# Windowed attention with its values as the stationary operand, in high and low parts, and outputs feature-major

## The chip, the cores and the metric

The kernel runs on one core of a Trainium2 chip. The metric is the device time of one execution in microseconds (us); the smaller is the better.

## The reference, cut to what matters

Two blocks follow each other on 512 tokens of 1024 features, all in fp32. The first ends in a large expert layer. The second begins with the layer that is changed here, a windowed attention with 16 heads of 64 features that share 4 key and value heads:

```python
u = rms_norm_2(h, norm_g[0])
q, k, v, z = jnp.split(u @ w_in, [1024, 1280, 1536], axis=-1)
logits = einsum(q, k) * scale - slopes * dist
logits = where(valid, logits, NEG_BIG)
probs = softmax(concatenate([logits, sink_col]))[..., :-1]
o = einsum(probs, v)
h = h + (o * silu(z)) @ w_out
```

A block of 128 queries sees its own block of 128 keys and the one on each side, so of four query blocks two see 2 key blocks and two see 3: 10 pairs of blocks per head. A gated embedding step and a second, different attention layer (called B below) follow.

## The kernel before

Almost every product of the kernel is fp32 split in a high and a low part of the type fp32r, and three matmuls (high by high, and two mixed ones) give the result. `linear_tm` and `linear_fm` are these products for a whole weight, in panels of two blocks of rows, which a helper loads, copies (`whi`, ACT, L148) and subtracts (`wlo`, L149). With `by_part` they run one output block at a time, in 24 matmuls of 512 columns (L153 to L155), and call `then` after each part. `to_fm` (L137 to L140) turns 128 tokens feature-major: eight transposes on TensorE (PE), in groups of four, each copied by ScalarE (ACT) and subtracted by VectorE (DVE).

A list scheduler with a timeline of its own fixes the order on every engine ahead of time; on the chip each engine works in its order, and waits there.

The stretches that matter here come in this order:

- **The tail.** The expert layer's last matmuls of token blocks 1 to 3 (`add_out`, L794 to L799, 512 columns each) end while VectorE and the others finish block 0. `make_u(t)` norms 128 tokens for layer A and turns them by `to_fm`. `make_u(0)` is called ahead of the tail (L860), `make_u(1)` and so on from inside it.
- **V, K and Q.** `linear_tm` for the values (into `vA`), `linear_fm` for the keys (`khA`, `klA`) and the first 8 heads' queries (`qA`).
- **Heads 0 to 7.** `linear_fm` for the other 8 heads' queries in four parts; after each, two heads.
- **Heads alone.** Heads 8 to 10, with what the scheduler leaves of the two heads before and takes of the next: the work of some five heads. So six are left in the three periods before, and five in the gates.
- **Gates.** `linear_tm` for z in eight parts of 24 matmuls, and after each of five parts a head. `gate_a` makes z times its sigmoid from a tanh (`th`), and multiplies it into `oA` (L1013).
- **Out.** `to_fm` of the four rows of `oA`, then the out projection.

One head is `a_head` (L951 to L990). For each of the four query blocks `t`: two matmuls give the logits (L965, L966, 384 or 256 columns, the PSUM tile `lg`), VectorE adds `abias` and takes the maximum (L969, the operation CUSTOM_DVE_ANT_0, into one of three buffers `L`), negates it (L972), ScalarE takes the exponential and its sum (L973), TensorE transposes each key block (L976, PSUM `tp`), one copy brings them to SBUF (`pt`: L979 on VectorE for odd blocks of the first 8 heads, otherwise L981 on ScalarE), and one fp32 matmul of 64 columns per key block (L983) has a block of `pt` as the stationary operand and `vA` as the moving one. So there are 10 transposes and 10 such matmuls per head, 160 and 160 in all, and each of these matmuls stands as two in the profile. At the end VectorE makes the reciprocal of the sums (L987, L988) and scales the head's four blocks with it into `oA` (L989), which is token-major.

Layer B's head (`b_head`, L1146 to L1176) does the last step in another way: its probabilities are split in `ph` and `pl` (L1163, L1164), its values are the stationary operand, high and low parts side by side, and 256 columns of probabilities move (L1170).

Of the kernel before, what the change touches and what calls it, by code (L numbers as in the profile page):

```python
# [91 lines left out]
def block_kernel(ctx: ExitStack, tc: tile.TileContext, A, out):  # L92
# [743 lines left out]
    for n in range(P):  # L836
# [17 lines left out]
        if n == P - WS - 1:  # L854
            assert turn == 2 * NSLOT
            g2 = ada_row(5)
            uT, make_u = normed_parts("norm_g_2", 0)
            nc.vector.tensor_mul(y, y, g2)
            nc.vector.tensor_add(x[:, 0], x[:, 0], y)
            make_u(0, "lg")  # L860

    for t in range(NG):
        for i, ops in enumerate(tail):
            add_out(t, ops, False, i == WS - 1)
        res = gp.tile([P, D], FT, name="res", tag="g", bufs=GB)
# [59 lines left out]
    klA = lz.tile([P, 4, S], FR, name="klA", tag="klA")  # L925
    vA = lz.tile([P, NT, 256], FT, name="vA", tag="vA")
    oA = lz.tile([P, NT, D], FT, name="oA", tag="oA")

# [17 lines left out]

    linear_tm(Wa, 8, 1280, 256, uT, NT, lambda t, p: nc.scalar.activation(vA[:, t], p, AF.Copy), by_part=True,
              then=lambda t: t == NT - 2 and make_u(NT - 1, "lg"))
    linear_fm(Wa, 8, 1024, 256, uT, NT, evac_ka)

    def a_head(h, q):  # L951
        abias = lw.tile([P, 3 * P], FT, name="abias")
        nc.vector.scalar_tensor_tensor(abias, dist[:, 0], -(2.0 ** (-8.0 * (h + 1) / 16.0)), dist[:, 1],
                                       op0=OP.mult, op1=OP.add)
        sm = small.tile([P, 3, NT], FT, name="sm3", tag="sm3")
        o = ps.tile([P, 512], FT, name="acc", tag="acc", bufs=4)
        for t in range(NT):
            sl = slice(t * P, (t + 1) * P)
            b_lo, b_hi = max(0, t - 1), min(NT - 1, t + 1)
            nb = b_hi - b_lo + 1  # L960
            n = nb * P
            c0 = (b_lo - (t - 1)) * P
            lg = ps.tile([P, 512], FT, name="lg", tag="lg")
            ks = slice(b_lo * P, (b_hi + 1) * P)
            nc.tensor.matmul(lg[:, :n], q[:, sl], khA[:, h // 4, ks], start=True, stop=False)  # L965
            nc.tensor.matmul(lg[:, :n], q[:, sl], klA[:, h // 4, ks], start=False, stop=True)  # L966
            L = lw.tile([P, 3 * P], FT, name="L", bufs=3)
            m = small.tile([P, 1], FT, name="m", tag="m")
            nc.vector.tensor_tensor_reduce(out=L[:, :n], in0=lg[:, :n], in1=abias[:, c0:c0 + n], scale=1.0,  # L969
                                           scalar=sink[:, h:h + 1], op0=OP.add, op1=OP.max, accum_out=m)  # L970
            nm = sm[:, 0, t:t + 1]
            nc.vector.tensor_scalar(nm, m, -1.0, None, op0=OP.mult)  # L972
            nc.scalar.activation(L[:, :n], L[:, :n], AF.Exp, bias=nm, accum_out=sm[:, 1, t:t + 1])  # L973
            p = ps.tile([P, 4, P], FT, name="tp", tag="tp")
            for b in range(nb):
                nc.tensor.transpose(p[:, b], L[:, b * P:(b + 1) * P], ident)  # L976
            pt = lw.tile([P, 3, P], FT, name="pt", bufs=3)
            if h < 8 and t % 2:
                nc.vector.tensor_copy(pt[:, :nb], p[:, :nb])  # L979
            else:  # L980
                nc.scalar.activation(pt[:, :nb], p[:, :nb], AF.Copy)  # L981
            for b in range(nb):
                nc.tensor.matmul(o[:, t * 64:(t + 1) * 64], pt[:, b],  # L983
                                 vA[:, b_lo + b, (h // 4) * 64:(h // 4 + 1) * 64], start=b == 0, stop=b == nb - 1)
# [46 lines left out]
    ple_split(0, lz.tile([P, 2, S], FT, name="pT", tag="vA"), pf)  # L1031
    _, make_n = normed_parts("ple_norm_g_2", 0, nT)
# [231 lines left out]
```

## Time and profile before

| | |
|---|---|
| time, median of 3 runs | 2329.86 us (2329.52 to 2330.2) |
| the profiled execution | 2336.29 us |
| its span | 2334.1 us |
| mean granted clock of TensorE | 0.984 |
| PE busy | 2241.3 us, 96% |
| DVE busy | 1623.3 us, 70% |
| ACT busy | 1114.2 us, 48% |
| POOL busy | 1051.2 us, 45% |

The span is what the profiler shows of the execution; 2.2 us lie around it. PE is TensorE, POOL GpSimd, SP the engine that issues most transfers. A matmul's duration in the rows overlaps the next one's, so two starts tell more than a duration. PEclk, or granted clock, is 1.00 at 2.4 GHz and 0.50 at 1.2 GHz.

### The profile page before, as it was taken

To read this page: it belongs to the slowest core of one execution; us is meant where nothing else is said; L and a number is where in the kernel's file an instruction comes from. 1 tells how busy PE (TensorE), PEld (TensorE's weight loads), DVE (VectorE), ACT (ScalarE), POOL (GpSimd) and SP (SyncE) were. 2 spreads that over 40 slices of the span, in tenths; PEclk is the share of its full clock that TensorE was granted. 3 is DMA by queue.
4 is the path that set the end of the run, shared out by engine and by line. 5 is a ranking of instruction groups with operands and counts; after the bars stand their busy time and mean duration, and the time that the engine had idled before them with its cause. 6 is when DMAs were issued, how large, how long until landed. Compare 5 with 4: busy or idle time off the path is not lost.

```text
span 2334.1 us, 32581 instructions
## 1 busy us (share of the span) xinstructions
PE 2241.3 (96%) x11610; PEld 1930.8 (83%) x11610; DVE 1623.3 (70%) x2962; ACT 1114.2 (48%) x2134; POOL 1051.2 (45%) x642
## 2 busy tenths in 40 slices
PE   7999999998999899999999999999999999989998
PEld 5777778988999899999997788887889789767676
DVE  7695447889585654888887988888565445347755
ACT  3656323436757675333332333333456444467742
POOL 4874034574545565778876655564110100121100
PEclk9999999999999999999999999999999999999999
DMA  7465122376767788999998999996410233211121
GB/s 277 145 204 184 60 77 79 124 236 207 257 244 259 247 297 308 341 342 342 334 336 303 340 327 342 327 336 234 129 39 18 82 108 97 74 49 53 33 82 63
DMA packets 206482, 463.04 MB, mean 198 GB/s; under 512 B 17680, under 2 KB 99056, under 8 KB 203248
## 3 DMA queue, kind: packets, MB, share of 16 engines
q1 hardware_dynamic: 169456, 326.72, 41.9%
q0 software_dynamic: 36864, 134.23, 15.8%
q8 instruction: 92, 1.51, 0.3%
q14 instruction: 70, 0.57, 0.1%
HBM read 415.26 MB, written 44.58 MB: 197 GB/s over the span
## 4 chain that ended last, share of the span: by engine, by line
PE 70%; DVE 9%; DMA 6%; issue 6%; POOL 4%; ACT 3%; SPq 0%; POOLq 0%; DVEq 0%; ACTq 0%
PE acc L155 16%; PE acc L154 16%; PE acc L153 15%; PE gp L680 3%; PE tp L155 2%; PE tp L154 2%; PE tp L153 2%; PE lg L154 2%; PE lg L153 2%; PE lg L155 2%; DMA g<-in_peer_v_dram,idx 2%; PE lg L1154 2%; DVE oh L666 1%; POOL wada L271 1%; POOL wlo L716 1%
## 5 line engine op out<-in xcount | busy, mean ns | idle before, releaser
L716 POOL TENSOR_TENSOR wlo<-wraw,whi 128x1024 fp32r<-128x1024 f32 x172 | 441.7, 2570 | 397.0 <-ACT whi L715 388.2
L715 ACT ACTIVATE whi<-wraw 128x1024 fp32r<-128x1024 f32 x256 | 268.9, 1051 | 153.5 <-PE lg L154 73.2
L153 PE MATMUL acc<-fm,whi 128*128 128x384 f32 (+2 forms) x932 | 333.3, 359 | 1.6 <-ACT av L728 1.3
L155 PE MATMUL acc<-fm,wlo 128*128 128x384 f32 (+2 forms) x932 | 322.5, 348 | 3.0 <-POOL wlo L716 2.9
L154 PE MATMUL acc<-fm,whi 128*128 128x384 f32 (+2 forms) x932 | 323.1, 347 | 0.0
L751 DVE CUSTOM_DVE_ANT_0 g<-g,h20y 128x1024 f32<-128x1024 f32 x128 | 197.5, 1548 | 120.5 <-DMA g<-in_peer_u_dram,idx 120.3
L790 ACT ACTIVATE wh<-w 128x384 fp32r<-128x384 f32 x128 | 67.2, 525 | 360.2 <-DVE w L787 345.1
L148 ACT ACTIVATE whi<-wraw 128x1024 fp32r<-128x1024 f32 (+5 forms) x142 | 138.4, 981 | 160.4 <-PE acc L155 89.2
L149 POOL TENSOR_TENSOR wlo<-wraw,whi 128x1024 fp32r<-128x1024 f32 (+4 forms) x48 | 104.4, 2183 | 240.1 <-ACT whi L148 231.5
L154 PE MATMUL acc<-wlo,wh 128*128 128x512 f32 x512 | 203.7, 398 | 5.1 <-POOL wlo L716 5.1
L761 DVE SCALAR_TENSOR_TENSOR h20y<-g,act,h20y 128x1024 f32<-128x1024 f32 x127 | 192.5, 1516 | 17.7 <-DMA g<-in_peer_v_dram,idx 17.2
L155 PE MATMUL acc<-whi,wl 128*128 128x512 f32 x512 | 204.0, 398 | 0.0
L153 PEld LDWEIGHTS acc<-fm,whi 128*128 128x128 f32 x932 | 178.3, 192 | 11.6 <-issue 2.2
L149 DVE TENSOR_TENSOR wlo<-wraw,whi 128x1024 fp32r<-128x1024 f32 (+3 forms) x94 | 109.2, 1169 | 113.1 <-ACT whi L148 109.5
L155 PEld LDWEIGHTS acc<-fm,wlo 128*128 128x128 f32 x932 | 177.7, 191 | 11.4 <-POOL wlo L716 4.2
L154 PEld LDWEIGHTS acc<-fm,whi 128*128 128x128 f32 x932 | 178.4, 192 | 9.0 <-issue 2.2
L734 POOL DMA_INDIRECT g<-in_peer_u_dram,idx x128 | 172.9, 1351 | 26.5 <-issue 14.5
L734 POOL DMA_INDIRECT g<-in_peer_v_dram,idx x128 | 160.7, 1255 | 34.6 <-issue 21.5
L153 PE MATMUL acc<-whi,wh 128*128 128x512 f32 x512 | 171.7, 396 | 0.5 <-ACT whi L715 0.4
L669 ACT ACTIVATE oh<-oh,gT 128x128 f32<-128x128 f32 x384 | 120.1, 392 | 77.4 <-DVE oh L666 77.2
L153 PE MATMUL acc<-whi,fm 128*128 128x512 f32 (+3 forms) x368 | 135.9, 375 | 3.3 <-ACT fm L139 2.1
L791 DVE TENSOR_TENSOR wl<-w,wh 128x384 fp32r<-128x384 f32 x128 | 113.2, 884 | 35.9 <-ACT wh L790 33.9
(367 smaller groups left out, 5512.8 us busy)
## 6 DMA issues: line engine op xcount, KB each, us to landing
wraw<-in_uT_dram SPq DMA_DIRECT2D x128, 512.0 KB
wraw<-in_peer_v_dram SPq DMA_DIRECT2D x128, 512.0 KB
wada<-in_w_adaT_dram SPq DMA_DIRECT2D x48, 512.0 KB
G_d<-stage SPq DMA_DIRECT2D x24, 1024.0 KB
gm<-G_d SPq DMA_DIRECT2D x64, 384.0 KB
A_d<-av SPq DMA_DIRECT2D x88, 192.0 KB
am<-A_d SPq DMA_DIRECT2D x88, 192.0 KB
wraw<-in_w_in_dram SPq DMA_DIRECT2D x24, 512.0 KB
```

Of the source, the lines that this page charges most:

```text
L148: nc.scalar.activation(hi[:, :nk, :n], raw[:, :nk, :n], AF.Copy)
L149: eng.tensor_sub(lo[:, :nk, :n], raw[:, :nk, :n], hi[:, :nk, :n].bitcast(FT))
L153: nc.tensor.matmul(o, lh, rh, start=first, stop=False)
L154: nc.tensor.matmul(o, lh, rl, start=False, stop=False)
L155: nc.tensor.matmul(o, ll, rh, start=False, stop=last)
L669: nc.scalar.activation(oh[:, 1, i], oh[:, 1, i], AF.Copy, scale=gT[:, q * 4 + i:q * 4 + i + 1])
L715: nc.scalar.activation(hi, raw, AF.Copy)
L716: eng.tensor_sub(lo, raw, hi.bitcast(FT))
L734: tc.keep_in_program_order(nc.gpsimd.indirect_dma_start(out=g, out_offset=None, in_=src, in_offset=bass.IndirectOffsetOnAxis(ap=idx0[:, s: ...
L751: nc.vector.tensor_tensor_reduce(out=g, in0=g, in1=h20, scale=1.0, scalar=0.0, op0=OP.mult, op1=OP.add, accum_out=act0[:, i:i + 1])
L761: nc.vector.scalar_tensor_tensor(y, g, act0[:, s:s + 1], y, op0=OP.mult, op1=OP.add)
L791: nc.vector.tensor_sub(wl, w, wh.bitcast(FT))
```

## The change

- `make_u(0)` moves from ahead of the tail into it, behind `add_out` of its second token block.
- The values are stored in two parts, high and low, 64 columns each side by side (`evac_va`): a ScalarE copy, and a VectorE subtraction that is new.
- In `a_head` two query blocks go together. All transposed probabilities are copied by ScalarE to `ph`, and VectorE subtracts them to `pl` (L992). A half head then takes six matmuls of type fp32r, two for each of three key blocks: values (128 columns, high and low) by `ph`, and values (64 columns, high) by `pl`, over 256, 128 and 256 moving columns. That is 12 per head and 192 in all.
- Their output is feature-major, high products on partitions 0 to 63, low ones on 64 to 127. ScalarE copies the upper half (`ol`), VectorE adds it to the lower into `oA`, now feature-major. The reciprocals go to `rs`, unapplied.
- `gate_a` multiplies `rs` into z instead of z into `oA`. `gated_a` transposes z (four transposes per 128 features, 32 in all) and multiplies it into `oA`. Eight ScalarE copies and eight VectorE subtractions then make the parts for the out projection, in place of `to_fm`, which had as many of each.
- `th` is now a buffer of the tag of the gains.

```diff
-            make_u(0, "lg")
 
     for t in range(NG):
         for i, ops in enumerate(tail):
             add_out(t, ops, False, i == WS - 1)
+        if t == 1:
+            make_u(0, "lg")
...
+    vA = lz.tile([P, NT, 4, P], FR, name="vA", tag="vA")
+    oA = lz.tile([P, 8, S], FT, name="oA", tag="oA")
+    rs = lz.tile([P, NT, A_HEADS], FT, name="rs")
+
+    def evac_va(t, p):
+        v = p.rearrange("p (h d) -> p h d", d=64)
+        nc.scalar.activation(vA[:, t, :, 0:64], v, AF.Copy)
+        nc.vector.tensor_sub(vA[:, t, :, 64:128], v, vA[:, t, :, 0:64].bitcast(FT))
...
+        for t0 in (0, 2):
+
+            b0 = max(0, t0 - 1)
+            ph, pl = [lw.tile([P, 3, 2 * P], FR, name=n) for n in ("ph", "pl")]
+            for t in (t0, t0 + 1):
...
+                nc.scalar.activation(ph[d], p[:, :nb], AF.Copy)
+                nc.vector.tensor_sub(pl[d], p[:, :nb], ph[d].bitcast(FT))
+
+            for i, (b, u0, u1) in enumerate(((0, 0, 2), (2, 1, 2), (1, 0, 2)) if t0 == 0 else
+                                            ((2, 0, 2), (1, 0, 1), (3, 0, 2))):
+                c, w = slice((t0 + u0) * P, (t0 + u1) * P), (slice(None), b - b0, slice(u0 * P, u1 * P))
+                v = vA[:, b, h // 4]
+                steps = [(o[:, c], v, ph[w]), (o[0:64, c], v[:, 0:64], pl[w])]
+                for n in ((0, 1), (1, 0))[i == 2]:
+                    nc.tensor.matmul(*steps[n], start=i == 0 and n == 0, stop=i == 2 and n == 0)
+        ol = tmp.tile([64, S], FT, name="ol", tag="h", bufs=2)
+        nc.scalar.activation(ol, o[64:128], AF.Copy)
+        nc.vector.tensor_add(oA[h % 2 * 64:h % 2 * 64 + 64, h // 2], o[0:64], ol)
         es = sm[:, 2]
         nc.scalar.activation(es, sm[:, 0], AF.Exp, bias=sink[:, h:h + 1])
         nc.vector.tensor_add(es, es, sm[:, 1])
-        nc.vector.reciprocal(es, es)
-        nc.vector.tensor_mul(oA[:, :, h * 64:(h + 1) * 64], o[:, :NT * 64].rearrange("p (t d) -> p t d", d=64),
-                             es[:, :, None].to_broadcast([P, NT, 64]))
+        nc.vector.reciprocal(rs[:, :, h], es)
...
-        th = lw.tile([P, 512], FT, name="th")
+        th = tmp.tile([P, 512], FT, name="th", tag="gain", bufs=2)
...
-            c = slice(j * 512, (j + 1) * 512)
-            nc.vector.tensor_mul(oA[:, i, c], oA[:, i, c], zA[:, i, c])
+            z = zA[:, i, j * 512:(j + 1) * 512].rearrange("p (h d) -> p h d", d=64)
+            nc.vector.tensor_mul(z, z, rs[:, i, 8 * j:8 * j + 8, None].to_broadcast([P, 8, 64]))
+
+    def gated_a(k):
+
+        p = ps.tile([P, 4, P], FT, name="tp", tag="tp")
+        for t in range(NT):
+            nc.tensor.transpose(p[:, t], zA[:, t, k * P:(k + 1) * P], ident)
+        nc.vector.tensor_mul(oA[:, k], oA[:, k], p.rearrange("p t s -> p (t s)"))
...
+                  then=lambda t, j=j: (one_head(11 + 4 * j + t), j and t < 2 and [gated_a(2 * t + i) for i in (0, 1)]))
+    for k in range(4, 8):
+        gated_a(k)
     aT = fm_whole()
-    for t in range(NT):
-        to_fm(oA[:, t], 8, aT, t)
+    for k in range(8):
+        nc.scalar.activation(aT[0][:, k], oA[:, k], AF.Copy)
+        nc.vector.tensor_sub(aT[1][:, k], oA[:, k], aT[0][:, k].bitcast(FT))
```

The scheduler makes a new order of it on every engine. Three places follow, in the order of issue.

TensorE, in the heads that stand alone, before: `lg` is a logit tile, `tp` a tile of transposes, L983 the fp32 product of probabilities and values.

```order
L965 MATMUL lg<-khA,qA 128x384
L966 MATMUL lg<-klA,qA 128x384
L976 MATMUL tp<-ident,L 128x128 x2
L983 MATMUL acc<-vA,pt 128x64 x3
L965 MATMUL lg<-khA,qA 128x256
L966 MATMUL lg<-klA,qA 128x256
L976 MATMUL tp<-ident,L 128x128 x2
L983 MATMUL acc<-vA,pt 128x64 x2
```

And after the change, where L1000 is the new product, and L978, L979 and L989 are the lines of the logits and transposes:

```order
L989 MATMUL tp<-ident,L 128x128 x4
L1000 MATMUL acc<-ph,vA 128x256
L978 MATMUL lg<-khA,qA 128x256
L979 MATMUL lg<-klA,qA 128x256
L978 MATMUL lg<-khA,qA 128x384
L979 MATMUL lg<-klA,qA 128x384
L1000 MATMUL acc<-pl,vA 64x256
L1000 MATMUL acc<-ph,vA 128x128
L1000 MATMUL acc<-pl,vA 64x128
L1000 MATMUL acc<-pl,vA 64x256
L1000 MATMUL acc<-ph,vA 128x256
L989 MATMUL tp<-ident,L 128x128 x6
```

The transposes now stand in groups of 4 and 6 in turn, and each group stands behind the five matmuls of a half head, of which three read `pl`.

VectorE, in the heads that stand alone, before, from a negation to the next head's `abias` (ISA is CUSTOM_DVE_ANT_0, and its second row reads the maximum out; L1008 is of the gates):

```order
L972 TENSOR_SCALAR sm_16113<-m 128x1
L969 ISA L,m<-lg,abias,sink 128x384
L969 ISA m 128x1
L969 ISA L,m<-lg,abias,sink 128x256
L969 ISA m 128x1
L1008 SCALAR_TENSOR_TENSOR zA<-th,zA 128x512
L989 TENSOR_TENSOR oA<-acc,sm_15987 128x4x64
L972 TENSOR_SCALAR sm_16113<-m 128x1 x2
L953 SCALAR_TENSOR_TENSOR abias<-dist 128x384
```

And after, where L1003 is the sum of the two halves of a head's output and L992 the subtraction to `pl`:

```order
L1003 TENSOR_TENSOR oA<-acc,ol 64x512
L985 TENSOR_SCALAR sm_15992<-m 128x1
L1007 RECIPROCAL rs<-sm_15992 128x4
L992 TENSOR_TENSOR pl<-tp,ph 128x3x128 x2
L982 ISA L,m<-lg,abias,sink 128x384
L982 ISA m 128x1
L982 ISA L,m<-lg,abias,sink 128x256
L982 ISA m 128x1
L992 TENSOR_TENSOR pl<-tp,ph 128x2x128
L985 TENSOR_SCALAR sm_16072<-m 128x1
L992 TENSOR_TENSOR pl<-tp,ph 128x2x128
L985 TENSOR_SCALAR sm_16072<-m 128x1
```

Between two heads' `abias` four subtractions are new, and the sum of 64x512 stands for the scaling of 4x64. The two subtractions of three blocks are the preceding head's, and stand ahead of the logits of blocks 2 and 3.

TensorE, in the tail, before: L137 with `h` is `make_u`'s transposes, here of block 0.

```order
L155 MATMUL acc<-whi,wl 128x512
L153 MATMUL acc<-whi,wh 128x512
L137 MATMUL tp<-ident,h 128x128 x8
L154 MATMUL acc<-wlo,wh 128x512
L155 MATMUL acc<-whi,wl 128x512
```

And after, at the tail's end and the first of the values' matmuls:

```order
L154 MATMUL tp<-wlo,wh 128x512
L155 MATMUL tp<-whi,wl 128x512
L137 MATMUL tp<-ident,h 128x128 x16
L153 MATMUL acc<-whi,fm 128x256
L154 MATMUL acc<-wlo,fm 128x256
```

Before, block 1's eight transposes alone stood there; now block 0's eight stand ahead of them.

## Rows read from the trace of the kernel before

**Rows 1.** Table by stretch: length, busy per engine (instructions), PEclk, DMA share, GB/s.
```profile
1628.00:1631.50 3.50, 3.50 (x11) 2.85 (x10) 1.96 (x3) 1.09 (x2) 0.00 (x0) 0.53 0.31 96
1705.50:1738.70 33.20, 31.18 (x206) 27.01 (x206) 20.85 (x79) 16.94 (x50) 0.00 (x0) 1.00 0.00 1
1746.00:1774.10 28.10, 26.24 (x179) 25.14 (x178) 21.14 (x82) 19.35 (x60) 5.21 (x3) 0.82 0.24 73
1751.00:1761.00 10.00, 9.83 (x45) 9.23 (x44) 6.33 (x23) 3.92 (x13) 0.46 (x1) 0.50 0.27 87
1774.10:1843.50 69.40, 68.59 (x399) 59.32 (x398) 30.77 (x98) 36.87 (x91) 9.77 (x4) 1.00 0.12 39
```

**Rows 2.** Timeline of TensorE in the stretch of heads alone: start, us, operation.
```profile
1765.14 0.49 PE L976 MATMUL tp<-ident,L 128*128 128x128 f32 x3
1765.46 0.78 PE L983 MATMUL acc<-vA,pt 128*128 128x64 f32 x6
1766.08 0.39 PE L976 MATMUL tp<-ident,L 128*128 128x128 f32 x2
...
1767.79 0.56 PE L983 MATMUL acc<-vA,pt 128*128 128x64 f32 x4
1768.18 0.50 PE L976 MATMUL tp<-ident,L 128*128 128x128 f32 x3
```

**Rows 3.** Timeline of VectorE in the same stretch.
```profile
1768.51 0.42 DVE L989 TENSOR_TENSOR oA<-acc,sm 128x256 f32<-128x256 f32 x1
...
1768.91 0.55 DVE L953 SCALAR_TENSOR_TENSOR abias<-dist 128x384 f32<-128x384 f32 x1
1769.37 0.48 DVE L969 CUSTOM_DVE_ANT_0 L<-lg,abias,sink 128x256 f32<-128x256 f32 x1
1769.78 0.08 DVE L969 DVE_READ_ACCUMULATOR2_ANT m<- 128x1 f32 x1
...
1770.05 0.61 DVE L969 CUSTOM_DVE_ANT_0 L<-lg,abias,sink 128x384 f32<-128x384 f32 x1
1770.59 0.08 DVE L969 DVE_READ_ACCUMULATOR2_ANT m<- 128x1 f32 x1
...
1773.27 0.55 DVE L953 SCALAR_TENSOR_TENSOR abias<-dist 128x384 f32<-128x384 f32 x1
```

**Rows 4.** Groups by line and form, 1700 to 2160 us: busy, mean ns, idle before.
```profile
L983 PE MATMUL acc<-vA,pt 128*128 128x64 f32 x320 | 45.0, 275 | 1.7 <-DVE pt L979 0.8 <-ACT pt L981 0.8
...
L1164 DVE TENSOR_TENSOR pl<-tp,ph 128x512 fp32r<-128x512 f32 x20 | 13.7, 687 | 2.2 <-ACT ph L1163 1.9
...
L1173 DVE TENSOR_TENSOR oB<-acc,ol 64x512 f32<-64x512 f32 x9 | 6.1, 683 | 13.7 <-ACT ol L1172 13.7
...
L979 DVE COPY pt<-tp 128x384 f32<-128x384 f32 x8 | 4.4, 555 | 0.1
```

**Rows 5.** Timeline of TensorE in a head of layer B.
```profile
2103.72 0.28 PE L1170 MATMUL acc<-ph,vB 128*128 128x256 f32 x1
2103.83 0.28 PE L1170 MATMUL acc<-pl,vB 128*64 128x256 f32 x1
```

**Rows 6.** Timeline of TensorE: its wait in the tail, and the first and the 13th of a run of matmuls.
```profile
1627.21 1.37 PE L137 MATMUL tp<-ident,h 128*128 128x128 f32 x8 [2.76 <-DVE h L228]
...
1634.14 0.40 PE L155 MATMUL acc<-whi,wl 128*128 128x512 f32 x1
...
1636.94 0.40 PE L155 MATMUL acc<-whi,wl 128*128 128x512 f32 x1
```

**Rows 7.** Timeline of TensorE: its two waits where the heads stand alone.
```profile
1748.85 0.38 PE L965 MATMUL lg<-khA,qA 128*128 128x256 f32 x1 [0.62 <-DVE m L969]
...
1750.42 0.63 PE L976 MATMUL tp<-ident,L 128*128 128x128 f32 x3 [1.07 <-ACT L L973]
```

**Rows 8.** Timeline of TensorE: its two waits between the gates and the out projection.
```profile
1845.46 0.50 PE L153 MATMUL acc<-whi,fm 128*128 128x512 f32 x1 [0.91 <-ACT fm L139]
...
1847.04 0.66 PE L137 MATMUL tp<-ident,oA 128*128 128x128 f32 x4 [0.86 <-DVE fm L140]
```

More of the change, by code (lines that the diff above doesn't have):

```diff
@@ L925, in block_kernel @@
     klA = lz.tile([P, 4, S], FR, name="klA", tag="klA")
-    vA = lz.tile([P, NT, 256], FT, name="vA", tag="vA")
-    oA = lz.tile([P, NT, D], FT, name="oA", tag="oA")
+    vA = lz.tile([P, NT, 4, P], FR, name="vA", tag="vA")
[5 more added lines that the diff above has]
+        nc.vector.tensor_sub(vA[:, t, :, 64:128], v, vA[:, t, :, 0:64].bitcast(FT))
     def evac_ka(m, p):
@@ L944, in evac_qa @@
             nc.vector.tensor_sub(qA[other, 2 * m + a], p[own], qA[own, 2 * m + a].bitcast(FT))
-    linear_tm(Wa, 8, 1280, 256, uT, NT, lambda t, p: nc.scalar.activation(vA[:, t], p, AF.Copy), by_part=True,
+    linear_tm(Wa, 8, 1280, 256, uT, NT, evac_va, by_part=True,
               then=lambda t: t == NT - 2 and make_u(NT - 1, "lg"))
@@ L956, in a_head @@
         o = ps.tile([P, 512], FT, name="acc", tag="acc", bufs=4)
-        for t in range(NT):
[L958 to L984, printed above, removed]
@@ new lines, in a_head @@
+        for t0 in (0, 2):
+            b0 = max(0, t0 - 1)
+            ph, pl = [lw.tile([P, 3, 2 * P], FR, name=n) for n in ("ph", "pl")]
+            for t in (t0, t0 + 1):
+                sl = slice(t * P, (t + 1) * P)
+                b_lo, b_hi = max(0, t - 1), min(NT - 1, t + 1)
+                nb = b_hi - b_lo + 1
+                n = nb * P
+                c0 = (b_lo - (t - 1)) * P
+                lg = ps.tile([P, 512], FT, name="lg", tag="lg")
+                ks = slice(b_lo * P, (b_hi + 1) * P)
+                nc.tensor.matmul(lg[:, :n], q[:, sl], khA[:, h // 4, ks], start=True, stop=False)
+                nc.tensor.matmul(lg[:, :n], q[:, sl], klA[:, h // 4, ks], start=False, stop=True)
+                L = lw.tile([P, 3 * P], FT, name="L", bufs=3)
+                m = small.tile([P, 1], FT, name="m", tag="m")
+                nc.vector.tensor_tensor_reduce(out=L[:, :n], in0=lg[:, :n], in1=abias[:, c0:c0 + n], scale=1.0,
+                                               scalar=sink[:, h:h + 1], op0=OP.add, op1=OP.max, accum_out=m)
+                nm = sm[:, 0, t:t + 1]
+                nc.vector.tensor_scalar(nm, m, -1.0, None, op0=OP.mult)
+                nc.scalar.activation(L[:, :n], L[:, :n], AF.Exp, bias=nm, accum_out=sm[:, 1, t:t + 1])
+                p = ps.tile([P, 4, P], FT, name="tp", tag="tp")
+                for b in range(nb):
+                    nc.tensor.transpose(p[:, b], L[:, b * P:(b + 1) * P], ident)
+                d = (slice(None), slice(b_lo - b0, b_hi - b0 + 1), slice((t - t0) * P, (t - t0 + 1) * P))
+                nc.scalar.activation(ph[d], p[:, :nb], AF.Copy)
[7 more added lines that the diff above has]
+                    nc.tensor.matmul(*steps[n], start=i == 0 and n == 0, stop=i == 2 and n == 0)
@@ L1011, in gate_a @@
         for i in done:
-            c = slice(j * 512, (j + 1) * 512)
-            nc.vector.tensor_mul(oA[:, i, c], oA[:, i, c], zA[:, i, c])
+            z = zA[:, i, j * 512:(j + 1) * 512].rearrange("p (h d) -> p h d", d=64)
+            nc.vector.tensor_mul(z, z, rs[:, i, 8 * j:8 * j + 8, None].to_broadcast([P, 8, 64]))
+    def gated_a(k):
+        p = ps.tile([P, 4, P], FT, name="tp", tag="tp")
+        for t in range(NT):
+            nc.tensor.transpose(p[:, t], zA[:, t, k * P:(k + 1) * P], ident)
+        nc.vector.tensor_mul(oA[:, k], oA[:, k], p.rearrange("p t s -> p (t s)"))
     def one_head(h):
@@ L1022, in block_kernel @@
         linear_tm(Wa, 8, 1536 + j * 512, 512, uT, NT, lambda t, p, j=j: gate_a(t, p, j),
-                  eng=nc.gpsimd, by_part=True, then=lambda t, j=j: one_head(11 + 4 * j + t))
+                  eng=nc.gpsimd, by_part=True,
+                  then=lambda t, j=j: (one_head(11 + 4 * j + t), j and t < 2 and [gated_a(2 * t + i) for i in (0, 1)]))
+    for k in range(4, 8):
+        gated_a(k)
     aT = fm_whole()
-    for t in range(NT):
-        to_fm(oA[:, t], 8, aT, t)
+    for k in range(8):
+        nc.scalar.activation(aT[0][:, k], oA[:, k], AF.Copy)
+        nc.vector.tensor_sub(aT[1][:, k], oA[:, k], aT[0][:, k].bitcast(FT))
     nT = [lz.tile([P, 8, S], FR, name=n, tag="qz", bufs=2) for n in ("nh", "nl")]
@@ L1030, in block_kernel @@
     pf = pf[:, 0], pf[:, 1]
-    ple_split(0, lz.tile([P, 2, S], FT, name="pT", tag="vA"), pf)
+    ple_split(0, lz.tile([P, 2, 2, S], FT, name="pT", tag="vA")[:, 0], pf)
     _, make_n = normed_parts("ple_norm_g_2", 0, nT)
```

## The prediction

> **What bounds the kernel now.** I read the share of each engine first (the table), then the table by stretch for the layer that changes, then the timelines of TensorE and VectorE inside it. TensorE is busy for 96% of the span, so the first guess is that matmuls taken away are time gained. The table by stretch shows where that holds [rows 1]. In the gates TensorE is busy for 68.59 of 69.40 us and VectorE for 30.77. With the heads 0 to 7 it is 31.18 of 33.20 in two periods (two parts of the linear, four heads). With the heads alone it is 26.24 of 28.10, but at a mean granted clock of 0.82: in 10 of these us it was 0.50, the 1.2 GHz level, so that 5 us went there. At full clock a head takes 1773.27 - 1768.91 = 4.36 us [rows 3], and TensorE has no gap in it.
>
> So TensorE is the bound, but narrowly where heads stand close: VectorE has 21.14 of 28.10 there [rows 1]. The change takes from TensorE and gives to VectorE, and the question is which of them ends a head.
>
> **TensorE's side.** A head's old product takes 0.62 us for a group of three key blocks (1765.46 to 1766.08) and 0.39 for two (1767.79 to 1768.18) [rows 2], so 2 x 0.62 + 2 x 0.39 = 2.02 us, and 32 us in all (the 320 rows of 275 ns [rows 4] overlap). The new one has 8 matmuls of 256 columns and 4 of 128 per head. Of 256 columns layer B has the very form: starts 0.11 to 0.12 us apart [rows 5], I take 0.117. Of 128 columns in fp32r the trace has none: at least half of that, 0.06; at most an old fp32 matmul, 0.62 / 3 = 0.21. I take 0.10, near the transposes, which move 128 columns and take 0.32 / 3 = 0.107 [rows 2]. That gives 0.94 + 0.40, and some 0.15 for changes between forms: 1.5 us. TensorE saves **0.5 us a head** (0.1 to 0.7 at the two bounds), 8 us in all. The Trainium skill ("TensorE: Matmul & The Clock Gate", section "Back-to-back issue gap") gives about 81 ns for a matmul of 128 columns in a stream of loads and matmuls; by it the 64 would cost 1.2 us less than by my 0.10, and no run here shows it.
>
> The transposes of z (32 in all) stand for those of `oA`: nothing. ScalarE gets the 16 copies that L979 made and 16 of `ol`; at some 0.55 and 0.7 us, after VectorE's rows of these sizes [rows 4], that is 1.3 us a head at most, where it was busy for 19.35 of 28.10 us with the heads alone and for half the gates [rows 1]. It stays behind VectorE.
>
> **VectorE's side.** Per head it has now, by starts [rows 3]: `abias` 0.46, two maxima over 256 at 0.41, two over 384 at 0.54, the scaling with a negation 0.40, and some 0.5 for three more negations, the sum and the reciprocal (my estimate): 3.3 us. The new `pl` reads the same PSUM tile as the copy of L979, which took 555 ns for 384 columns; layer B's same subtraction took 687 for 512 [rows 4], and on the line through both 256 take 423. Less 0.08 of overlap (the scaling has 0.42 us, and the next starts within 0.34 to 0.40): 0.47 and 0.34, twice each, **1.62 us**. The sum of the halves, 64x512, took 683 ns in layer B [rows 4], 0.60 net, for the scaling's 0.34. A head then needs 3.3 + 1.6 + 0.3 = **5.2 us of VectorE**, against 4.36 - 0.5 = 3.9 of TensorE. In heads 0 to 7 the copies of L979 go (0.8 a head), so there the growth is 1.1.
>
> **Heads alone.** VectorE is now the bound. By the order shown ahead, the logits of blocks 2 and 3 need an `L` that a group of four transposes frees; these stand behind five matmuls that read `pl`. From the first large subtraction's end this is 0.1 + 5 x 0.11 + 0.3 + 0.15, about 1.0 us, of which the second subtraction covers 0.5. A second such place costs 0.2. So a head takes 5.2 + 0.7 = 5.9 us. Five heads at full clock: 29.5 us against 28.1. But TensorE then works 3.9 of 5.9 us. Before this, waits of 0.62 and 1.07 us [rows 7] came just ahead of the fall to 0.50 [rows 1]; they end in VectorE's maximum and in the exponential behind it, so the longer VectorE makes them no shorter. I take the same 10 us at half clock. There a head is bound by TensorE at 2 x 3.9 = 7.8 us: 10 us hold 1.3 heads, the other 3.7 take 21.8, and the start costs 1 us. 32.8 against 28.1: **+4.5** (0 to +11).
>
> **Heads 0 to 7.** A period of 16.6 us holds 23 or 24 matmuls of the linear, 5.5 us [rows 6], and two heads. TensorE saves 1.0. VectorE had 20.85 of 33.20 us [rows 1], 10.4 a period, and gets 2.2 more; during the linear it soon lacks logits, since three `L` are all there are, so some 2.5 of these 5.5 us are lost for it. 12.6 + 2.5 + two bubbles of 0.7 = 16.5. **0** (-3 to +3 for three periods).
>
> **Gates.** Matmuls of 512 columns start (1636.94 - 1634.14) / 12 = 0.233 us apart [rows 6], so a part is 24 x 0.233 = 5.6 us; the stretch holds eight parts and five heads, a part with a head takes (69.40 - 3 x 5.6) / 5 = 10.5 us, and TensorE is hardly ever free [rows 1]. VectorE has room on average (30.77 us of 69.40, and 1.9 x 5 more). But a head's operations stand between two groups of 24 matmuls, in a chain: transposes, copy to `ph` (ACT), subtraction, five matmuls, next transposes. From four transposes on it is 0.15 + 0.4 + 0.4 + 0.3 of waits and 0.55 of matmuls, then 1.7 from a maximum to the six transposes: some 5 us where TensorE has 3.9 to do and had 4.4. Per part +0.2: **+1** (-2.5 to +4; -2.5 if the linear's VectorE time takes the chain out, 5 x 0.5). `rs` into z replaces z into `oA` at equal size; the eight products of `gated_a`, 0.69 us each after the 512 columns of rows 4, fall in the last parts, where VectorE has that room, and behind them.
>
> **The tail.** Before, TensorE waited 2.76 us for block 0's norm [rows 6], and 3.5 us at a clock of 0.53 [rows 1] cost 1.65 more: 4.4 us that go. Block 0's eight transposes now stand behind the tail, just ahead of block 1's eight. There are only two `lg` tiles for the four groups, so block 1's two wait until ScalarE has copied and VectorE subtracted (687 ns for 512) block 0's: 0.15 + 0.6 + 2 x 0.7 = 2.1 us, and as VectorE has both blocks' sums and norms ahead of it, 3 to 4. **-0.5** (-4 to +1; +1 if the clock falls there again, as it fell behind the old wait).
>
> **The rest.** `vA`'s four subtractions lie beside 96 matmuls of the values; if that cover were gone, 1.7 us. Before the out projection TensorE waited 0.91 and 0.86 us [rows 8] for the first parts of `oA`. Now it waits for the last gates' transposes, `gated_a`'s product and the new copies, but the first four of the eight feature blocks are done earlier: **0** (-1.5 to +1). The gains' loads go behind the out projection's panels on SP's queue, because `th` holds their buffers; their reader, the next norm, comes behind 96 matmuls and more of the out projection, 22 us. Cover gone, that norm waits, by at most the longest wait seen here, 2.76 us [rows 6].
>
> **Sum:** 4.5 + 0 + 1 - 0.5 + 0 = +5.0 us. The profiled execution of 2336.29 us (span 2334.1) would be 2341.3. It stands 6.4 us above the median of 2329.86, so the median becomes **2334.9**. A measurement of this kernel can tell about 0.2%, 4.7 us; the forecast lies at that edge.
>
> **Rivals.**
>
> 1. *TensorE remains the bound* (faster). The scheduler's order lets VectorE work ahead in the linears' time, and with other gaps the fall of the clock doesn't come. Then the 11 heads beside linears save 0.5 us each (-5.5), the heads alone take 29.5 + 1 instead of 28.1 (+2.4), the tail gives 4: 2329.9 - 7.1 = 2322.8. For it: VectorE has only 63% of the time with heads 0 to 7, and the gates' 44% [rows 1]. Against it: the chain through `pl` is longer than the one through `pt`, and the place from which it decides is whether TensorE's waits in a part stay under 0.5 us.
> 2. *The savings pay for the heads alone* (no change). As forecast there (+4.5) and in the tail (-0.5), but the 11 heads beside linears gain 0.3 us each (-3.3): 2330.6. For it: TensorE had no idle time in the gates to hide a saving in.
> 3. *The clock stays down* (slower). If TensorE works 3.9 of 5.9 us, it may fall to half again each time it is back: all five heads at 7.8 us are 39 + 1 against 28.1, +12, and the sum is 2342. For it: in the 10 us at 0.50 [rows 1] the engine was 98% busy, and it fell after waits far shorter in sum than those to come. Against it: the 33.20 us with heads 0 to 7 hold 2.0 us of idle time at a clock of 1.00 [rows 1]. The Trainium skill (the same page, section "HAM oscillation — how this bites in real kernels") says that a loop of short matmul bursts with a wait in each can lose its clock in every pass; by it this rival is what comes, and the trace so far shows both kinds.
>
> **How the numbers follow.** The forecast has 0.35, of which 0.07 falls within 0.2%; rival 1 has 0.20, rival 2 0.27, rival 3 0.18. So: faster 0.20, same 0.34, slower 0.46. The range leaves out a part of rivals 1 and 3: 2322 to 2343. The likeliest case's own range, between 2331 and 2339, has the bounds of heads alone and gates half each.
>
> **What would show it.** Right: in the heads alone VectorE busy nearly throughout and TensorE idle for 1.5 us or more of each head, a head at 5.5 to 6.3 us at full clock, waits of L1000 for `pl`; granted clock 0.50 for 10 us or so there; parts of the gates at 10.2 to 10.9 us; a wait of 2 to 4 us in the sixteen transposes behind the tail, and none ahead. Wrong: a head alone at under 5 us, or gates' parts under 10 (rival 1); a clock of 0.5 through the heads (rival 3); 128 columns in fp32r at over 0.2 us. And a stall at the first norm behind the out projection would show that the gains' loads were not covered.

## The result, and the profile after

The changed kernel takes 2350.48 us (median of 7 runs, 2346.25 to 2361.66) against 2330.2 before in the same comparison: **slower, by a ratio of 1.0078, 95% interval 1.0060 to 1.0096**. Forecast were 2334.9 and a range up to 2343.

The profiled execution took 2352.14 us, its span is 2349.9, 15.8 longer than before. The table by stretch of the changed kernel, with bounds at the same places as in [rows 1]: from the first head's matmul to the end of the last part of the queries' linear; the heads alone; the gates; and all three. Columns: bounds, length, then busy time and instructions of PE, PEld, DVE, ACT and POOL, the granted clock, the DMA share, GB/s.

```profile
1690.55:1749.00 58.45, 52.19 (x278) 40.32 (x277) 38.99 (x136) 38.24 (x101) 5.78 (x3) 0.97 0.07 19
1749.00:1780.57 31.57, 24.84 (x146) 18.76 (x145) 27.36 (x98) 24.44 (x70) 6.07 (x3) 0.95 0.23 67
1780.57:1857.92 77.35, 70.16 (x364) 56.12 (x364) 43.16 (x120) 39.76 (x95) 10.32 (x4) 0.98 0.12 35
1690.55:1857.92 167.37, 147.19 (x785) 115.20 (x784) 109.50 (x352) 102.44 (x263) 22.17 (x9) 0.97 0.12 35
```

The same view of the kernel before, for the first of these and for all three:

```profile
1692.88:1746.03 53.15, 50.92 (x323) 44.16 (x322) 33.44 (x121) 30.75 (x82) 6.64 (x3) 1.00 0.08 22
1692.88:1843.51 150.63, 145.73 (x897) 128.62 (x896) 85.36 (x300) 86.98 (x231) 21.59 (x9) 0.97 0.13 40
```

So heads 0 to 7 took 58.4 us for 53.2, the heads alone 31.6 for 28.1, the gates 77.4 for 69.4: +5.3, +3.5 and +8.0, 16.7 in all. Sixteen of the transposes of z, some 1.4 us by their starts, now lie within the gates; the transposes of `oA` that they stand for came behind [rows 8]. What lies ahead of the first head ended 2.3 us earlier (1690.55 for 1692.88), which says little: in the profiles of the second, third and fourth experiment, which are alike up to there, it ended between 1687.2 and 1693.2. What follows the gates took 1.4 more.

TensorE is free for 20.2 us of the three stretches, before for 4.9; VectorE has 24 us more to do. TensorE's largest wait there is for VectorE's maximum, which frees a logit tile (engine, line, waited for: us in total, times, longest):

```profile
PE lg L978 <- DVE m L982: 8.7, 19, 1.5
```

All that it waits for other engines adds up to 19.5 us, and all but 2.6 of that (for ScalarE's `ph`) end in VectorE. The new product itself waits only 2.2 us for `pl`.

The chip granted 1.2 GHz for part of the heads alone, but for less time than before [rows 1], some 3 us for 10. It did so for some 3 us in each of the two other stretches as well, where the clock had been 1.00 before: once behind TensorE's waits of 0.76, 0.45 and 0.71 us, and once behind one of 1.45. From 1765 us on TensorE ran at 1.00 with a wait in every half head:

```profile
1735.00:1740.00 5.00, 3.63 (x15) 2.81 (x16) 3.95 (x16) 3.06 (x9) 0.00 (x0) 0.67 0.00 0
1755.00:1760.00 5.00, 4.19 (x21) 3.33 (x22) 4.25 (x16) 3.40 (x12) 0.66 (x1) 0.72 0.54 167
1765.00:1770.00 5.00, 3.92 (x27) 3.00 (x27) 4.51 (x18) 3.95 (x12) 0.00 (x0) 1.00 0.00 0
1825.00:1830.00 5.00, 4.62 (x15) 3.93 (x16) 4.09 (x11) 2.30 (x7) 2.15 (x1) 0.66 0.73 195
```

VectorE's timeline in one head alone, from one `abias` to the next (start, duration, line, operation, and in brackets the idle time before it and what ended it):

```profile
1772.12 0.55 DVE L962 SCALAR_TENSOR_TENSOR abias<-dist 128x384 f32<-128x384 f32 x1
...
1774.78 0.99 DVE L992 TENSOR_TENSOR pl<-tp,ph 128x384 fp32r<-128x384 f32 x2
1776.31 0.62 DVE L982 CUSTOM_DVE_ANT_0 L<-lg,abias,sink 128x384 f32<-128x384 f32 x1 [0.54 <-PE tp L989]
...
1778.04 0.55 DVE L962 SCALAR_TENSOR_TENSOR abias<-dist 128x384 f32<-128x384 f32 x1
1778.86 0.48 DVE L982 CUSTOM_DVE_ANT_0 L<-lg,abias,sink 128x256 f32<-128x256 f32 x1 [0.26 <-PE tp L989]
```

A head is 1778.04 - 1772.12 = 5.92 us, against 4.36 in [rows 3]; the three ahead of it took 7.58, 6.79 and 6.20 by the same starts. VectorE is busy but for two waits, 0.54 behind the large subtractions and 0.26 behind `abias`. Both end with the transposes that free an `L`.

TensorE's timeline of a half head's product, which answers to [rows 2] and [rows 5]:

```profile
1777.85 0.28 PE L1000 MATMUL acc<-pl,vA 128*64 128x256 f32 x1
1777.96 0.22 PE L1000 MATMUL acc<-ph,vA 128*128 128x128 f32 x1
1778.02 0.34 PE L1000 MATMUL acc<-pl,vA 128*64 128x128 f32 x2
1778.20 0.29 PE L1000 MATMUL acc<-ph,vA 128*128 128x256 f32 x1
1778.33 0.82 PE L989 MATMUL tp<-ident,L 128*128 128x128 f32 x6
```

A matmul of 256 columns is followed after 0.11 to 0.13 us, one of 128 after 0.06. Five take 0.48 us, a head's twelve 2 x (0.48 + 0.12) = 1.2, where the old product took 2.02 [rows 2].

In the gates, VectorE at the end of its work in a part of the linear and at its next operation:

```profile
1792.48 0.52 DVE L992 TENSOR_TENSOR pl<-tp,ph 128x384 fp32r<-128x384 f32 x1
1792.92 0.14 DVE L985 TENSOR_SCALAR sm<-m 128x1 f32<-128x1 f32 x1
1797.85 0.62 DVE L982 CUSTOM_DVE_ANT_0 L<-lg,abias,sink 128x384 f32<-128x384 f32 x1 [4.79 <-PE tp L989]
```

And TensorE beside it, the first of the 24 matmuls, the first of the head behind them, the transposes, and the first of the next 24:

```profile
1791.13 0.39 PE L153 MATMUL acc<-whi,fm 128*128 128x512 f32 x1
...
1796.72 0.28 PE L978 MATMUL lg<-khA,qA 128*128 128x256 f32 x1
...
1797.43 0.60 PE L989 MATMUL tp<-ident,L 128*128 128x128 f32 x4
...
1802.72 0.39 PE L153 MATMUL acc<-whi,fm 128*128 128x512 f32 x1
```

VectorE works 1.9 us into the part, has then filled its three `L`, and waits 4.79 us for transposes that stand behind the 24 matmuls. Then TensorE has a head, 6.0 us long with some 3.6 us of work in it (an estimate: the prediction's 3.9, less 0.3 for the cheaper product), because what it needs now goes through VectorE. So a part with its head takes 1802.72 - 1791.13 = 11.59 us: 4.79 in which VectorE waits, and 6.8 of its work, one behind the other. Three parts of the queries' linear and the five parts of the gates that a head follows each have such a wait, of 3.9 to 5.2 us, and together these are 38.4 of the 44.8 us below. The waits of VectorE for the transposes over the three stretches (engine, line, waited for: us in total, times, longest), after and then before:

```profile
DVE L L982 <- PE tp L989: 44.8, 21, 5.2
```

```profile
DVE L L969 <- PE tp L976: 3.9, 5, 2.0
```

Before, VectorE waited about as long in sum, but for logits (26.4 us) and for the transposes of its copies (14.0): it had little to do, and TensorE hardly had to wait for it (4.9 us free).

In the tail, the sixteen transposes and the wait inside them, in TensorE's timeline:

```profile
1635.88 1.03 PE L137 MATMUL tp<-ident,h 128*128 128x128 f32 x8
...
1639.63 1.25 PE L137 MATMUL tp<-ident,h 128*128 128x128 f32 x8 [2.71 <-DVE fm L140]
```

The wait of 2.76 us ahead of block 0's transposes [rows 6] is gone, and this one is new. From 1641 to 1645 us the granted clock was 0.57, as it was 0.53 behind the old wait.

### The profile page after: what moved, and what is told of

It is laid out like the page before. It is cut to its first block, busy times and chain, and to the rows that moved or that the text cites. A ratio compares the mean times of both kernels' runs of the same rounds, so it can differ in the third digit from the quotient of the medians.

```text
span 2349.9 us, 32380 instructions
## 1 busy us (share of the span) xinstructions
PE 2239.0 (95%) x11482; PEld 1913.2 (81%) x11482; DVE 1647.4 (70%) x3022; ACT 1129.4 (48%) x2166; POOL 1059.0 (45%) x642
## 4 chain that ended last, share of the span: by engine, by line
PE 69%; DVE 13%; DMA 5%; issue 5%; POOL 5%; ACT 4%; SPq 0%; POOLq 0%; DVEq 0%; ACTq 0%
PE acc L153 15%; PE acc L154 15%; PE acc L155 15%; PE gp L680 3%; PE lg L153 2%; PE lg L154 2%; PE lg L155 2%; PE tp L155 2%; PE tp L154 2%; PE tp L153 2%; PE lg L1183 2%; POOL wlo L716 2%; DVE oh L666 1%; DMA wada<-in_w_adaT_dram 1%; POOL wada L271 1%
## 5 line engine op out<-in xcount | busy, mean ns | idle before, releaser
L716 POOL TENSOR_TENSOR wlo<-wraw,whi 128x1024 fp32r<-128x1024 f32 x172 | 448.3, 2609 | 395.7 <-ACT whi L715 393.8
L791 DVE TENSOR_TENSOR wl<-w,wh 128x384 fp32r<-128x384 f32 x128 | 118.1, 923 | 36.0 <-ACT wh L790 32.3
```

The source lines that it names most:

```text
L716: eng.tensor_sub(lo, raw, hi.bitcast(FT))
L791: nc.vector.tensor_sub(wl, w, wh.bitcast(FT))
```

## The experiments

Each comparison has its own runs of the kernel before. "The stretch" is from the first head to the last gate: 150.6 us before, 167.4 after.

**The moved norm alone.**

```diff
+            make_u(0, "lg")
...
-        if t == 1:
-            make_u(0, "lg")
```

> The changed kernel with make_u(0) back ahead of the tail; all else as changed. Theory T (taking turns: with three L buffers VectorE can't go on with a head during a part of the linear, since the transposes that free them stand behind its 24 matmuls): the 18 us come from the heads, so this stays at 2345 to 2353. Rival M (the moved norm costs): back to 2333 to 2338.

Measured: 2349.2 us, ratio 1.0062 (1.0042 to 1.0083). It overlaps the changed kernel's 1.0060 to 1.0096: the move is worth nothing that shows here. The stretch is 166.9 us long, as with the move. The slowdown is in the heads.

**Without the low part.**

```diff
-                nc.vector.tensor_sub(pl[d], p[:, :nb], ph[d].bitcast(FT))
...
-                steps = [(o[:, c], v, ph[w]), (o[0:64, c], v[:, 0:64], pl[w])]
...
+                nc.tensor.matmul(o[:, c], v, ph[w], start=i == 0, stop=i == 2)
```

> The changed kernel without pl: the subtraction on VectorE (4 a head) and the 6 matmuls a head that read it are left out, so the low part of the probabilities is missing from the output. Rival V (VectorE's added work alone sets the time, 1.62 us a head): a head alone falls from 5.9 to some 4.0 us, heads beside linears lose the same, 16 x 1.6 = 26 us: about 2324. Theory T: the heads alone fall in the same way (5 x 1.9), but beside a linear VectorE still stops at the third L, so the parts lose only the chain's 0.5 to 1.0 us: 2332 to 2340.

Measured: 2321.94 us, ratio 0.9941 (0.9912 to 0.9970). The table by stretch, for the whole stretch and for 5 us of its heads alone:

```profile
1687.18:1831.09 143.91, 131.14 (x689) 104.72 (x688) 88.38 (x288) 100.22 (x263) 21.34 (x9) 0.98 0.14 41
1757.00:1762.00 5.00, 4.50 (x30) 3.36 (x29) 4.19 (x18) 4.86 (x15) 0.00 (x0) 1.00 0.00 0
```

VectorE's work falls from 109.5 to 88.4 us and the stretch by 23.5, more than the 21.1 taken off. This is rival V's number, not T's: the low part costs 1.5 us a head on average, beside the linears too (7.1 us with heads 0 to 7, 5.4 in the heads alone, 11.0 in the gates). But the edit takes out a step of the chain (transposes, `ph`, `pl`, values) and 96 of TensorE's matmuls together with VectorE's work, so it doesn't tell load from chain. In the heads alone ScalarE is next, busy for 4.86 of 5 us: a head takes 1761.57 - 1756.94 = 4.63 us by VectorE's `abias`, still more than before.

**Five `L` buffers.**

```diff
-        abias = lw.tile([P, 3 * P], FT, name="abias")
+        abias = lw.tile([P, 3 * P], FT, name="abias", bufs=1)
...
-                L = lw.tile([P, 3 * P], FT, name="L", bufs=3)
+                L = lw.tile([P, nb * P], FT, name="L%d" % nb, bufs=5 - nb)
```

> The changed kernel with five L buffers (two of 384 columns, three of 256) in place of three, with one abias buffer in place of two to make room; no arithmetic changes. Theory T: VectorE works ahead during the linear, its wait on the transposes (4.8 us in each part) mostly goes, and a part of the gates with its head falls from 11.6 to 10.0 to 10.5 us, a period of heads 0 to 7 from 17.9 to 15.5 to 16.5: 2332 to 2340. Rival V: VectorE's work is the same, so under 3 us are gained: 2345 to 2351.

Measured: 2338.72 us, ratio 1.0016 (0.9997 to 1.0034): 10 to 14 us come back, with not one operation less (10.5 against the first run, which has the same comparison; 14 by the two ratios). The stretch is 9.0 us shorter: 3.5 with heads 0 to 7, 1.1 in the heads alone, 4.4 in the gates. Stretch and wait:

```profile
1690.62:1849.04 158.42, 141.18 (x786) 112.22 (x785) 111.31 (x353) 101.96 (x263) 22.22 (x9) 0.99 0.13 39
```

```profile
DVE L L982 <- PE tp L989: 4.0, 5, 1.5
```

VectorE's work is the same (111.3 us); its wait for the transposes fell from 44.8 to 4.0, and all its idle time from 57.9 to 47.1. Load alone can't be the cause.

**`abias` on GpSimd.**

```diff
-        nc.vector.scalar_tensor_tensor(abias, dist[:, 0], -(2.0 ** (-8.0 * (h + 1) / 16.0)), dist[:, 1],
-                                       op0=OP.mult, op1=OP.add)
+        nc.gpsimd.tensor_scalar(abias, dist[:, 0], -(2.0 ** (-8.0 * (h + 1) / 16.0)), None, op0=OP.mult)
+        nc.gpsimd.tensor_add(abias, abias, dist[:, 1])
```

> The changed kernel with abias made by GpSimd (a product and a sum in place of VectorE's one operation), which is idle there. It takes 0.46 us a head from VectorE. Rival V: 16 x 0.46 = 7 us are gained: about 2343. Theory T: 0.46 us in the heads alone (5 heads, 2 us), little beside a linear, where VectorE idles anyway: 2346 to 2350.

Measured: 2348.3 us, ratio 1.0058 (1.0032 to 1.0083); its interval overlaps the changed kernel's. The 7 us of rival V did not come. VectorE still waited for the transposes much as before, and GpSimd took 1.23 and 1.02 us for what VectorE does in 0.55:

```profile
DVE L L982 <- PE tp L989: 40.9, 19, 5.1
```

```profile
L962 POOL TENSOR_SCALAR abias<-dist 128x384 f32<-128x384 f32 x14 | 17.3, 1234 | 72.0 <-DVE m L982 48.0 <-DVE sm L985 24.0
...
L963 POOL TENSOR_TENSOR abias<-abias,dist 128x384 f32<-128x384 f32 x14 | 14.3, 1021 | 1.1
```

Taking this work from VectorE gained nothing that can be told. As `abias` itself takes four times as long now, this is a weaker test of VectorE's load than the third run.

**A woven order.** `linear` calls a hook behind each three matmuls, a head is a generator that gives one step per call, and TensorE's instructions are held in the order of the program.

```diff
+                if mid:
+                    mid(m, k)
...
+    def pe(ins):
+        return tc.keep_in_program_order(ins) if pins[0] else ins
...
+        logits(0)
+        yield
+        logits(1)
+        yield
+        split(0)
+        logits(2)
+        yield
+        split(1)
+        logits(3)
+        yield
+        values(0)
+        split(2)
+        yield
+        split(3)
+        yield
+        yield
+        values(2)
```

> The changed kernel with TensorE's order written by hand where the heads are: behind every three matmuls of the linear stands one piece of a head (the logits of a block, the transposes of another, the values' matmuls of a half), a head begins every 4.4 such threes, all 16 beside linears and none alone; five L buffers. The same arithmetic. Theory T (engines take turns in the changed order): from the first head to the last gate 12 parts of 5.6 us and 16 heads of 3.6 are all that TensorE has to do, 125 us against 167 measured; I expect 130 to 145, so 2313 to 2330 in all. Rival V (the work of VectorE and ScalarE per head is the limit, in any order): VectorE has some 16 x 5.1 + 17 = 99 us, so it can't be the limit in a woven order, but if its waits are, the stretch stays over 155 us and the time over 2338.

> The same hand-written order with the three L buffers of the change. If the buffers matter only because the transposes that free them stood behind 24 matmuls (T), it is within 5 us of the order with five. If three buffers are the limit by themselves, it is 10 us or more slower than with five.

Measured: 2350.33 us (1.0057, 1.0037 to 1.0077) with five `L`, 2351.86 (1.0069, 1.0048 to 1.0090) with three. The buffers no longer matter, as T said, but the 2313 to 2330 that T said for the order did not come: the stretch is 171.8 us long. **Theory T falls as the whole cause.** Stretch, TensorE's timeline, and VectorE's beside it:

```profile
1699.69:1871.50 171.81, 140.60 (x791) 113.50 (x790) 122.29 (x356) 106.01 (x267) 21.40 (x9) 0.96 0.13 38
```

```profile
1747.66 0.38 PE L1017 MATMUL acc<-ph,vA 128*128 128x256 f32 x1 [0.24 <-ACT ph L1005]
1750.59 0.33 PE L1017 MATMUL acc<-pl,vA 128*64 128x256 f32 x1 [2.55 <-DVE pl L1006]
```

```profile
1747.59 2.47 DVE L969 SCALAR_TENSOR_TENSOR abias<-dist 128x384 f32<-128x384 f32 x1
1749.99 0.55 DVE L1006 TENSOR_TENSOR pl<-tp,ph 128x384 fp32r<-128x384 f32 x1
```

These values' matmuls, of a head's first half, stand one three (0.7 us and a step) behind the last transposes whose `pl` they read, and `pl` comes through two engines, each with other work in its queue. TensorE waits at the head of its queue, and the linear behind it waits too. Its largest wait in the stretch:

```profile
PE acc L1017 <- DVE pl L1006: 12.5, 11, 2.5
```

With 6.0 us for `ph` and 4.5 that the profile puts down to VectorE's next operation, the values wait 23.0 us, and all of it in the first halves. The second halves stand two threes behind their last transposes, and at none of the 16 does the profile show a wait:

```profile
1753.32 0.63 PE L1003 MATMUL tp<-ident,L 128*128 128x128 f32 x2
...
1756.49 0.28 PE L1017 MATMUL acc<-ph,vA 128*128 128x256 f32 x1
1756.61 0.28 PE L1017 MATMUL acc<-pl,vA 128*64 128x256 f32 x1
```

**The old product in the same order.** The kernel before, woven in the same way, with five `L`; `values` is the old product of one block, two threes behind that block's transposes.

> The kernel of before (old product, outputs token-major, norm ahead of the tail) with the same hand-written order and five L buffers. If the new product's saving on TensorE is real (2.02 against 1.2 to 1.3 us a head by the traces, 16 x 0.75 = 12 us) and only the order hid it, this is 8 to 14 us slower than the woven changed kernel. If the woven order alone is the gain and VectorE's extra work eats the saving, both are within 5 us.

Measured: 2329.75 us, ratio 0.9967 (0.9949 to 0.9985): 20 us *faster* than the woven new product, which neither case of the expectation held. Two things differ, though: the old chain has one copy in it, and each of its products stands two threes behind its transposes, where the new one's first halves stand one behind. At two threes the new product did not wait either. So these 20 us don't show what the longer chain costs; the old product at one three was not run. The stretch:

```profile
1696.01:1843.33 147.32, 141.78 (x909) 126.02 (x908) 98.30 (x305) 90.44 (x235) 21.48 (x9) 0.99 0.15 46
```

**The steps further apart.** The theory was now that the chain is too long for the distances (C). First the values go three threes behind the last transposes that they read, in place of one and two (the expectation's three counts from the first ones); with them the logits of two blocks move, and the output's tile is taken later:

```diff
-        o = ps.tile([P, 512], FT, name="acc", tag="acc", bufs=4)
...
         split(0)
-        logits(2)
         yield
         split(1)
+        logits(2)
+        yield
         logits(3)
         yield
-        values(0)
         split(2)
         yield
+        o = ps.tile([P, 512], FT, name="acc", tag="acc", bufs=4)
+        values(0)
         split(3)
         yield
         yield
+        yield
         values(2)
```

> The woven changed kernel again, with the steps of a head further apart: the transposes of a block two threes behind its logits, as before, but the values' matmuls three threes behind the transposes whose low part they read, in place of one or three. The woven order with one three between them gained nothing (2350), and TensorE waited there for pl and ph. If the length of the chain transposes, ph on ScalarE, pl on VectorE, values is what TensorE waits for (theory C), the stretch from the first head to the last gate falls from 172 to 140 to 152 us, so 2322 to 2334 in all. If VectorE's load of some 6 us a head with what else it does (rival V) sets the rate, it stays within 6 us of the first woven order: 2344 to 2354.

Measured: 2338.26 us, ratio 1.0023 (1.0002 to 1.0044), between the two cases. The values no longer wait for `ph` or `pl`, and the stretch fell by 15.4 us:

```profile
1691.72:1848.17 156.45, 133.68 (x791) 110.40 (x790) 118.78 (x356) 104.88 (x267) 22.01 (x9) 0.99 0.14 42
```

Now TensorE's largest wait is the one whose distance had been left:

```profile
PE tp L1002 <- ACT L L990: 15.3, 17, 2.5
```

Then the transposes too, three threes behind their logits, and a head begins every 4.25 threes in place of 4.4 (the two were not tried apart):

> The woven changed kernel with the steps further apart once more: transposes three threes behind their logits instead of two, and the values' matmuls three threes behind the transposes they need; a head begins every 4.25 threes. Theory C: TensorE's waits of 20 us on the exponential shrink to under 8, the stretch from 156 to 142 to 150 us: 2324 to 2333 in all. Rival V (VectorE, 15.6 of 20 us busy in that stretch, and ScalarE with 14 now pace it): the stretch stays at 153 to 158 us: 2335 to 2341.

Measured: **2328.49 us, ratio 0.9975 (0.9959 to 0.9991)**, as theory C said. That wait went from 15.3 to 3.8 us, all of TensorE's waits at these transposes from 20.4 to 14.2 (the largest now for `pl`), and the stretch from 156.5 to 149.4, with all the work of the change in it:

```profile
PE tp L1002 <- DVE pl L1005: 5.2, 6, 1.2
PE tp L1002 <- ACT L L990: 3.8, 3, 2.6
```

```profile
1691.49:1840.92 149.43, 132.68 (x791) 113.69 (x790) 118.98 (x356) 104.10 (x267) 21.89 (x9) 0.97 0.15 44
```

**Five `L` in the kernel before**, the same edit as in the third run.

> The kernel of before with the five L buffers (and one abias) of the third run. There VectorE's copy and TensorE's product follow each other without a subtraction between, and TensorE was the bound beside the linears. If three buffers became too few only with the change, this is within 3 us of before; if more L help any kernel of this form, 6 to 12 us faster.

Measured: 2329.93 us against 2333.2, ratio 0.9981 (0.9961 to 1.0002): within its uncertainty of no change; 3.3 us by the medians, just past the first case. Its profile shows where a gain would lie, in the heads alone:

```profile
1743.19:1766.16 22.97, 21.76 (x185) 21.23 (x184) 20.62 (x86) 19.31 (x60) 5.24 (x3) 1.00 0.29 90
```

The stretch is 145.5 us, 5.1 shorter than before, and all of that lies in the heads alone, which took 28.1 us at a granted clock of 0.82 [rows 1] and here 23.0 at 1.00. Whether the buffers kept the clock up, one profile can't tell. Beside the linears both stretches are within 0.7 us of before: there three buffers became too few with the change.

## Why the prediction was wrong

The sign was right, and VectorE as what ends a head; the size was not: +5.0 us forecast, 14 to 22 by the interval. What failed is the overlap beside the linears: with heads 0 to 7 VectorE was to lose 2.5 us of each linear part, and lost 4.7 to 5.2.

- *Heads alone*: the mechanism was right. 5.9 us a head were worked out, 5.92 measured; the two waits as 0.5 and 0.2, measured 0.54 and 0.26. TensorE was to idle for 1.5 us of a head and did for some 1.1. The stretch: +4.5 forecast (its terms, 32.8 less 28.1, give 4.7), +3.5 measured. That these are so near is in part luck: the clock was low for some 3 us, not 10, and three heads took 6.2 to 7.6 us.
- *TensorE's side*: 0.10 us for a matmul of 128 columns was 0.06, the lower bound, and 1.5 us a head was 1.2. The saving was 0.8 us a head, not 0.5, and it was worth nothing that shows, as TensorE waited for VectorE.
- *Heads 0 to 7*: forecast 0, measured +5.3. The step that failed is "some 2.5 of these 5.5 us are lost" for VectorE during the linear: in the three parts where it waited, 5.04, 5.20 and 4.71 were lost.
- *Gates*: forecast +1, measured +8.0, the largest error, by the same step. VectorE idled for 3.9 to 5.0 us of each linear part, so most of a head's work on it came between the parts, and the step "some 5 us where TensorE has 3.9 to do" (its written terms add up to 3.5) was 6.0 in the part shown; that part with its head took 11.59 us, and 10.7 were forecast. Some 1.4 of the 8.0 are the transposes of z. I had read VectorE's room off an average. The three `L` and the transposes that free them stood in the order ahead of the prediction; I used them for the heads alone and not for the parts. The third run shows the price: 10 to 14 us of the time, 9.0 of the stretch.
- *The clock beside the linears*: no term, as it had been 1.00 there. It was low for some 3 us in each of the two stretches, worth up to 1.7 us each by the rows at 0.67 and 0.66 (an estimate).
- *The tail*: -0.5 forecast, with a new wait of 2 to 4 us (2.71 measured), and +1 if the clock fell again (it did). The first run can't tell it from zero.
- *The rest*: 0 forecast, +1.4 in one profile, within the scatter of runs. The largest wait for a load of gains behind the gates is 1.6 us, as before.
- *Rival 1* assumed that VectorE would work ahead in the linears. That was the question, and the answer was no. *Rival 3*'s clock did not come, though its time was nearer: from 1765 us on, with waits of 0.25 to 0.82 us in every half head, it was not lost in any pass.

Behind the size stand two things. One is the order, which let the engines take turns while three `L` were all there were (10 to 14 us by the third run). The other is the distance between the steps of a head: with more of it the woven kernel gained some 20 us, and came back to the time of before with all its work. That the new chain, longer by one engine, needs more distance than the old is argued and not shown, as both products were free of waits at two threes. What stays open, too, is why the scheduler put whole parts together; its costs were not examined. How the gain of the third run divides between `L` and the single `abias` was not tried.

## What to carry to other kernels

A product that saves TensorE time but puts a second engine between transposes and matmuls lengthens a chain. In an order that each engine must follow, ask first how many instructions stand between a step and the one that needs it, and how many buffers let the engine behind go on meanwhile. An average of busy time over a stretch says nothing of that: look for what the engine needs at the moment when the long block of the other begins. Here the same operations took 171.8 or 149.4 us by the places of the steps. And compare like with like: the new product at its best (0.9975) is no faster than the old one in a woven order (0.9967) or with five `L` alone (0.9981). It spends on waits what it saves: TensorE is free for 16.8 us of its best stretch, and for 5.5 in the old product's.

## What was not expected of the hardware

VectorE's `abias`, 0.55 us alone, took 2.47 in the woven run (shown there). GpSimd was subtracting a panel at that time, in its timeline:

```profile
1747.30 2.35 POOL L149 TENSOR_TENSOR wlo<-wraw,whi 128x1024 fp32r<-128x1024 f32 x1 [44.76 <-ACT whi L148]
```

`abias` reads two operands in SBUF, as GpSimd did, and ended soon after it. In the changed kernel `pl`, with one operand in PSUM, kept its 0.42 us for 256 columns beside the same subtractions, and `abias` did not keep its 0.55 (GpSimd, then VectorE):

```profile
1747.99 4.71 POOL L149 TENSOR_TENSOR wlo<-wraw,whi 128x1024 fp32r<-128x1024 f32 x2
```

```profile
1751.14 0.42 DVE L992 TENSOR_TENSOR pl<-tp,ph 128x256 fp32r<-128x256 f32 x1
...
1751.55 1.58 DVE L962 SCALAR_TENSOR_TENSOR abias<-dist 128x384 f32<-128x384 f32 x1
```

The Trainium skill ("SBUF — State Buffer", section "SBUF: two separate sides") says that an operation of VectorE with two inputs in SBUF and a GpSimd operation that reads SBUF hold a shared pair of ports by turns, for a whole instruction. The rows of `abias` agree: in the woven run it took 1.9 us longer, most of GpSimd's 2.35.

The clock: with TensorE idle for over 1 us of each 5.92 from 1765 us on, it stayed at 1.00 in the heads alone of the changed kernel. It fell to 0.57 behind the single wait of 2.71 us in the tail, and to 0.66 behind one of 1.45 us in the gates.
